# Block 0's expert values weighted on ScalarE and summed on GpSimd, with a fourth tile for its gathered rows

## The chip, the cores and the metric

The kernel runs on one core of a Trainium2 chip. A core has five engines that work side by side, each with its own in-order queue of instructions: TensorE (PE in the profile; its weight loads are PEld), VectorE (DVE), ScalarE (ACT), GpSimd (POOL) and SyncE (SP). SyncE issues the plain DMAs here; GpSimd issues the indirect ones, which gather rows of a table by an index. The metric is the device time of one execution in microseconds, lower is better.

## The reference

One transformer block on 1024 tokens of width 1024, in float32:

```
h  = rmsnorm(x);  x = x + token_mixers(h)      # retention and RWKV-7, gated and merged
h2 = rmsnorm(x);  x = x + peer(h2)             # 16384 experts, 8 heads x 16 chosen a token
x  = x + sigmoid(rmsnorm(x) @ w_gate) * (p @ w_up)
out = rmsnorm(x)
```

The change lies in `peer`. A token's queries give scores against two sets of 128 sub-keys for each head; the best 16 of each set are paired, the best 16 pairs are the head's experts, and a softmax gives their gates. So each token has 128 expert numbers and gates:

```
act = gelu(einsum('td,tkd->tk', h2, expert_u[ids]))     # 128 rows of u for each token
out = einsum('tk,tkd->td', gates * act, expert_v[ids])  # 128 rows of v for each token
```

## The kernel before

Tokens go in eight blocks of 128, a token to a partition. The projections (`project_*`, names Pw, Pr, Pg in the profile), the recurrences (R and T: RWKV pairs and retention, in four units of 256 tokens), the merge of the branches (M), the output matmul (O), the second norm (N) and the queries (F) come in the order of a string in `cfg` (L857). For each block b there are three steps of the expert layer:

- `choose(b)` and `select` (S, L829 to L926): scores are loaded in four parts, two at a time, VectorE takes the best 16 by `max`, `max_index` and `match_replace`, builds the candidates, and picks out the indices with one-hot tiles. Score parts, candidates and one-hots all use the tag `oh` of the pool `sel`, two tiles of 2 KB a partition.
- `dots(b)` (D, L936): for k from 0 to 127 GpSimd gathers row `ids[:, k]` of u into a tile of 4 KB a partition, and VectorE multiplies it with h2 and sums (L956). After the last row the gelu and gates give the weights t.
- what is done with the rows of v: for blocks 0, 6 and 7 `direct()` (G, L988) gathers them in the same way and VectorE adds `t[:, k] * u` to x (L1003), where x starts as the residual. For the other blocks the whole table v is streamed through TensorE against a matrix of the weights (`groups` W, `stream` V).

The gathered rows go round over the tiles that `row(k)` (L975) finds in `self.places`: three in the pool `up` at first; one more (`ux`, L1039) when `open_first` runs, at `<` in the order; two more (`um`, L1021) when the table is streamed. When the stream is over, `values` takes `ux` away again (L1204).

The order string puts the first stage as `[1 x1 S0 r S1 T1 R2 T2 R3 T3 G0 g D1 ]`. `G0` means `dots(0, True)`: D0, then the 128 rows of G0. A planner orders each engine's queue: it takes instructions by their place in the program, those earlier first, when it reckons that what they need is ready. So the rows of D0 and G0 fill gaps between the recurrences R and T, which come before them, and go ahead of the gate projection `g`. `M1 O1 N1 F1` of the next stage follow D1 in the program, and the key choice S2 needs the scores of F1.

At the end, block 7's rows of v are fetched: the first `cfg["ahead"]` of 128 before the last part of the table is streamed (L1185), the others in seven groups, each planned after one of seven tail blocks is done (L1209 to L1211). A tail block (L) is a norm, a matmul with the gate weights `wt`, and the final norm; `wt` is loaded into room that is free when the stream's matrices and the pool of `ux` are closed (`open_tail`, L1230). The tail of block 7 comes last.

```
def row(self, k):
    k %= sum(n for _, n in self.places)
    for pool, n in self.places:
        if k < n:
            return pool.tile([P, D], F32, tag="u", name=self.nm("u"), bufs=n)
        k -= n
```

Of the kernel before, what the change touches and what calls it, by code (L numbers as in the profile page):

```python
# [9 lines left out]
F32 = mybir.dt.float32  # L10
# [10 lines left out]
P = 128  # L21
# [82 lines left out]
class Builder:  # L104
# [724 lines left out]
    def choose(self, b):  # L829

        self.ph = f"S{b}"
        tv = self.sel.tile([P, 8, 2, 16], F32, tag="tv", name=self.nm("tv"), bufs=1)
        ti = self.sel.tile([P, 8, 2, 16], U32, tag="ti", name=self.nm("ti"), bufs=1)
        for h in range(0, 8, 2):
            sc = self.sel.tile([P, 2, 2, 128], F32, tag="oh", name=self.nm("sc"), bufs=2)
            self.q.dma_start(sc, self.scd[b, :, h:h + 2])
            for k in range(2):
                for c in range(2):
                    self.top16(tv[:, h + k, c, :], ti[:, h + k, c, :], sc[:, k, c, :])
        self.select(b, tv, ti)  # L840

    def top16(self, v, i, s):

# [9 lines left out]
    BOXES = [(0, 1, 16), (1, 3, 8), (4, 4, 4), (8, 8, 1)]  # L853
    cfg = dict(nv=5, parts=((0, 256), (256, 768)), mq=0, wp1=(512, 4, 4), mf=((0, 256), (256, 256), (512, 512)),
               wp2=(512, 4, 3), nu=3, nab=3, lag=1, aact=(1, 2), wide=1, hp=(), nmid=1, nmore=2, lb=2, nk=4,
               units=((128, 256), (384, 384)), tail=(0, 1, 2, 6, 3, 4, 5, 7), ahead=64,
               order="[0 c r x0 T0 g k + ] { M0 O0 N0 F0 } [1 x1 S0 r S1 T1 R2 T2 R3 T3 G0 g D1 ] "  # L857
                     "{ M1 O1 N1 F1 ( M2 S2 O2 } < N2 S3 F2 D2 W ) ",
               later=("D3 S4 D4 S5 D5", "S6 S7 G6 G7"))

    def select(self, b, tv, ti):
        self.ph = f"S{b}"
        nc, wk = self.nc, self.sel
        V = nc.vector

        def t(tag, dt, shape=(8, 16)):
            return wk.tile([P, *shape], dt, tag=tag, name=self.nm(tag), bufs=2 if tag == "oh" else 1)

        cand = t("oh", F32, (8, 64))
        o = 0  # L870
        for i0, ni, nj in self.BOXES:
            sh = [P, 8, ni, nj]
            V.tensor_add(cand[:, :, o:o + ni * nj].rearrange("p h (i j) -> p h i j", i=ni),
                         tv[:, :, 0, i0:i0 + ni, None].to_broadcast(sh), tv[:, :, 1, None, 0:nj].to_broadcast(sh))
            o += ni * nj
        tih = t("tih", F16, (2, 16, 8))
        V.tensor_copy(tih, ti.rearrange("p h c n -> p c n h"))
        bv, bp = t("bv", F32), t("bp", I32)
        for h in range(8):
            self.top16(bv[:, h, :], bp[:, h, :].bitcast(U32), cand[:, h, :])  # L880

        m, n = t("m", I32), t("n", I32)
        rank = t("rank", F16, (2, 16, 8))
        turned = [rank[:, c].rearrange("p k h -> p h k") for c in range(2)]
        V.tensor_scalar(m, bp, 3, None, op0=ALU.logical_shift_right)
        V.tensor_scalar(n, bp, 2, None, op0=ALU.logical_shift_right)
        V.scalar_tensor_tensor(m, n, -5.0, m, op0=ALU.add, op1=ALU.max)
        V.scalar_tensor_tensor(m, bp, -47.0, m, op0=ALU.add, op1=ALU.max)
        V.tensor_scalar(turned[0], m, -1.0, 0.0, op0=ALU.add, op1=ALU.max)
        V.tensor_scalar(m, bp, 16.0, -8.0, op0=ALU.is_ge, op1=ALU.mult)  # L890
        V.tensor_scalar(n, bp, 40.0, -4.0, op0=ALU.is_ge, op1=ALU.mult)
        V.tensor_add(m, m, n)
        V.tensor_scalar(n, bp, 56.0, -3.0, op0=ALU.is_ge, op1=ALU.mult)
        V.scalar_tensor_tensor(m, n, 15.0, m, op0=ALU.add, op1=ALU.add)
        V.tensor_tensor(m, bp, m, op=ALU.bitwise_and)
        V.tensor_copy(turned[1], m)

        ijf = t("ijf", F32, (2, 8, 16))
        sh = [P, 8, 16, 8]
        i16 = self.iota16[:, None].to_broadcast(sh)  # L900
        for c in range(2):
            for kk in (slice(0, 8), slice(8, 16)):
                oh = t("oh", F32, (8, 64)).rearrange("p a b -> p (a b)").bitcast(F16)
                oh = oh.rearrange("p (k n h) -> p k n h", k=8, n=16)
                V.tensor_tensor(oh, rank[:, c, kk, None, :].to_broadcast(sh), i16, op=ALU.is_equal)
                V.tensor_mul(oh, oh, tih[:, c, None].to_broadcast(sh))
                for w in (8, 4, 2):
                    V.tensor_add(oh[:, :, 0:w], oh[:, :, 0:w], oh[:, :, w:2 * w])
                V.tensor_add(ijf[:, c, :, kk].rearrange("p h k -> p k h"), oh[:, :, 0], oh[:, :, 1])
        ijf = ijf.rearrange("p c h k -> p c (h k)")  # L910

        gt, s8 = t("gt", F32), t("s8", F32, (2, 8))
        V.tensor_sub(gt, bv, bv[:, :, 0:1].to_broadcast([P, 8, 16]))
        nc.scalar.activation(gt, gt, AF.Exp)
        V.tensor_reduce(s8[:, 0], gt, axis=AX.X, op=ALU.add)
        V.reciprocal(s8[:, 1], s8[:, 0])
        V.tensor_mul(gt, gt, s8[:, 1, :, None].to_broadcast([P, 8, 16]))

        ids = t("ids", I32, (128,))
        V.scalar_tensor_tensor(ids, ijf[:, 0], 128.0, ijf[:, 1], op0=ALU.mult, op1=ALU.add)  # L920
        rows = slice(b * 128, b * 128 + 128)
        self.q.dma_start(self.idsd[rows, :], ids)
        self.q.dma_start(self.gated[rows, :], gt.rearrange("p h k -> p (h k)"))
        self.q.dma_start(self.ijd[rows], ijf)
        self.dump("ids", ids, lambda d: d[rows, :])
        self.dump("gates", gt.rearrange("p h k -> p (h k)"), lambda d: d[rows, :])  # L926
# [61 lines left out]
    def direct(self):  # L988

        b, ids, t = self.gather  # L990
        nc, up = self.nc, self.up
        V = nc.vector
        rows = slice(b * 128, b * 128 + 128)
        table = self.i["peer_v"][0]
        self.ph = f"G{b}"
        x = up.tile([P, D], F32, tag="u_h2", name=self.nm("u_x"), bufs=1)
        self.q.dma_start(x, self.x1d[rows, :])
        for k in range(128):
            self.ph = f"G{b}"
            u = self.row(k)  # L1000
            nc.gpsimd.indirect_dma_start(out=u, out_offset=None, in_=table,  # L1001
                                         in_offset=bass.IndirectOffsetOnAxis(ap=ids[:, k:k + 1], axis=0))
            V.scalar_tensor_tensor(x, u, t[:, k:k + 1], x, op0=ALU.mult, op1=ALU.add)  # L1003
            if k == 127:
                self.dump("x2", x, lambda d: d[rows, :])
                if b == S // 128 - 1:
                    self.x2[b] = x
                else:
                    self.q.dma_start(self.x2d[rows, :], x)
            yield  # L1010
# [290 lines left out]
    def mixers(self):  # L1301
# [6 lines left out]
        for step in self.cfg["order"].split():  # L1308
            op, k = step[0], int(step[1:] or 0)
            with self.tc.high_priority() if step in self.cfg["hp"] else ExitStack():  # L1310
# [15 lines left out]
                elif op == "(":  # L1326

                    self.rctx.close()
                    self.wide = self.cfg["wide"]
                    last = ExitStack()  # L1330
                    self.open_weights(last, self.nm("wp2"), *self.cfg["wp2"])
                    last.push(self.open_big("left"))
                elif op == "<":
                    self.first = self.open_first()
                elif op == ")":
                    last.close()
                elif op == "W":
                    self.build(0, (0,))
                elif op in "]}":
                    pools.close()  # L1340
                elif op == "w":
                    self.project_rwkv()
                elif op == "x":
                    for p in range(4):
                        self.project_rwkv(self.RWKV_CTS[3 * p + (2 if p else 0):3 * p + 5])
                        self.rwkv_pair(k, p)
                elif op == "r":
                    self.project_ret(range(8))
                elif op == "g":
                    self.project_gates(range(16))  # L1350
                elif op == "R":
                    self.rwkv(k)
                elif op == "Q":
                    self.rwkv_pair(k // 10, k % 10)
                elif op == "T":
                    self.retention(k)
                elif op == "M":
                    mT[k] = self.branches(k)
                elif op == "O":
                    xs[k] = self.w_out(k, mT[k])  # L1360
                elif op == "N":
                    h2T[k] = self.norm2(k, xs[k])
                elif op == "F":
                    self.queries(k, h2T[k])
                elif op == "S":
                    self.choose(k)
                else:
                    self.dots(k, op == "G")
        self.pctx.close()
        self.up_ctx = up  # L1370
        return up
# [34 lines left out]
```

## Time and profile before

| | |
|---|---|
| median of 3 runs | 3992.57 us (3992.57 to 3999.76) |
| profiled execution | 4005.58 us, span 4003.8 us |
| TensorE busy | 3216.1 us (80%) |
| VectorE busy | 3067.7 us (77%) |
| ScalarE busy | 984.8 us (25%) |
| GpSimd busy | 1665.9 us (42%) |
| mean granted TensorE clock | 0.884 |
| HBM | 1057.5 MB read, 61.7 MB written, 280 GB/s over the span |

Busy times are summed over the span; they say how full an engine is on average, not what ends last in a stage. The granted clock is a share of full speed. The chain of waits, followed back from the last instruction, gives 20% of the span to "issue", 13% to GpSimd, 13% to DMA, 8% to VectorE and 4% to TensorE. In names, `D0.u` is a gathered row of u for block 0, `G0.u` one of v, `G0.u_x` the sum x.

### The profile page before, as it was taken

How to read it: one execution, taken by the hardware profiler on the slowest of the kernel's cores; microseconds unless marked ns; L12 is line 12 of the kernel's file. 1: busy time of each engine (PE TensorE's matmuls, PEld its weight loads, DVE VectorE, ACT ScalarE, POOL GpSimd, SP SyncE). 2: the span in 40 equal slices, each digit the busy share in tenths (PEclk: the TensorE clock that was granted, in tenths of full speed). 3: DMA queues.
4: the chain of work that ended last, by engine and by line, in shares of the span. 5: the costliest groups of instructions: out<-in, count | busy, mean ns of one | idle time of the engine just before them, and what ended most of it. 6: DMA issues, size and time to landing. Idle time of an engine off the chain costs nothing.

```text
span 4003.8 us, 50659 instructions
## 1 busy us (share of the span) xinstructions
PE 3216.1 (80%) x17036; PEld 2383.0 (60%) x17036; DVE 3067.7 (77%) x7212; ACT 984.8 (25%) x2059; POOL 1665.9 (42%) x1416
## 2 busy tenths in 40 slices
PE   6997768997998876586666975379889998999396
PEld 6886647887888765455554432257654555666142
DVE  5663587886887777687778889989898888676576
ACT  5432342211232210121336001323252222000021
POOL 0000013323233233312554456866537767676442
PEclk8998879998999977798886987589989999999698
DMA  6336548778777768976996999899949999999864
GB/s 193 111 100 189 183 160 260 225 241 262 238 246 228 253 197 272 342 242 225 313 332 211 415 381 357 306 353 409 368 167 369 382 377 383 397 416 395 333 222 163
DMA packets 517257, 1122.57 MB, mean 280 GB/s; under 512 B 42946, under 2 KB 280708, under 8 KB 516996
## 3 DMA queue, kind: packets, MB, share of 16 engines
q0 software_dynamic: 202752, 738.29, 50.8%
q1 hardware_dynamic: 314244, 381.05, 27.6%
q8 instruction: 134, 2.20, 0.2%
q14 instruction: 127, 1.04, 0.1%
HBM read 1057.49 MB, written 61.67 MB: 280 GB/s over the span
## 4 chain that ended last, share of the span: by engine, by line
issue 20%; POOL 13%; DMA 13%; DVE 8%; PE 4%; ACT 0%; SPq 0%; POOLq 0%; DVEq 0%; ACTq 0%
DMA D3.u<-in_peer_u_dram,D3.u_ids 4%; DMA G7.u<-in_peer_v_dram,D7.u_ids 2%; POOL D6.u L954 2%; POOL D7.u L954 2%; POOL D2.u L954 2%; POOL D5.u L954 2%; POOL G6.u L1001 2%; POOL D4.u L954 2%; DVE D3.u L956 1%; DMA D5.u<-in_peer_u_dram,D5.u_ids 1%; PE D7.acc L1164 1%; PE O2.mm L296 1%; POOL G7.u L1001 1%; DMA D4.u<-in_peer_u_dram,D4.u_ids 1%; POOL D1.u L954 1%
## 5 line engine op out<-in xcount | busy, mean ns | idle before, releaser
L1164 PE MATMUL D7.acc<-V1.v,M.M 128*128 128x512 f32 x1536 | 671.1, 598 | 1.3 <-DMA V1.v<-in_peer_v_dram 1.3
L1164 PEld LDWEIGHTS D7.acc<-V1.v,M.M 128*128 128x128 f32 x1536 | 372.9, 244 | 281.9 <-issue 178.4
L1164 PE MATMUL D5.acc<-V0.v,M.M 128*128 128x512 f32 x1024 | 461.2, 611 | 45.7 <-DMA V0.v<-in_peer_v_dram 43.6
L954 POOL DMA_INDIRECT D0.u<-in_peer_u_dram,D0.u_ids x128 | 134.7, 1052 | 827.6 <-DMA D0.u_ids<-idsd 539.5
L1164 PEld LDWEIGHTS D5.acc<-V0.v,M.M 128*128 128x128 f32 x1024 | 251.0, 247 | 245.3 <-issue 130.0
L1001 POOL DMA_INDIRECT G0.u<-in_peer_v_dram,D0.u_ids x128 | 133.5, 1043 | 277.9 <-DVE G0.u_x L1003 197.8
L954 POOL DMA_INDIRECT D2.u<-in_peer_u_dram,D2.u_ids x128 | 143.5, 1121 | 240.6 <-DVE D2.u L956 114.4
L954 POOL DMA_INDIRECT D6.u<-in_peer_u_dram,D6.u_ids x128 | 190.8, 1491 | 123.6 <-DVE K5.raw L1067 38.9
L954 POOL DMA_INDIRECT D1.u<-in_peer_u_dram,D1.u_ids x128 | 131.8, 1030 | 233.1 <-DVE D1.u L956 153.9
L1001 POOL DMA_INDIRECT G7.u<-in_peer_v_dram,D7.u_ids x128 | 151.3, 1182 | 164.1 <-DVE L1.rsq L326 52.0
L1086 PEld LDWEIGHTS <-W0.A 128*128 128x128 bf16 x1536 | 100.7, 139 | 199.3 <-issue 105.7
L956 DVE SCALAR_TENSOR_TENSOR D1.u<-D1.u,D1.u_h 128x1024 f32<-128x1024 f32 x128 | 156.4, 1223 | 78.1 <-DMA D1.u<-in_peer_u_dram,D1.u_ids 72.7
L956 DVE SCALAR_TENSOR_TENSOR D7.u<-D7.u,D7.u_h 128x1024 f32<-128x1024 f32 x128 | 156.4, 1226 | 64.8 <-DMA D7.u<-in_peer_u_dram,D7.u_ids 54.3
L956 DVE SCALAR_TENSOR_TENSOR D0.u<-D0.u,D0.u_h 128x1024 f32<-128x1024 f32 x128 | 155.9, 1221 | 57.2 <-DMA D0.u<-in_peer_u_dram,D0.u_ids 55.2
L954 POOL DMA_INDIRECT D4.u<-in_peer_u_dram,D4.u_ids x128 | 175.5, 1371 | 57.3 <-issue 31.7
L1003 DVE SCALAR_TENSOR_TENSOR G7.u_x<-G7.u,D7.u_t,G7.u_x 128x1024 f32<-128x1024 f32 x128 | 164.5, 1285 | 45.1 <-DMA G7.u<-in_peer_v_dram,D7.u_ids 40.2
L954 POOL DMA_INDIRECT D3.u<-in_peer_u_dram,D3.u_ids x128 | 137.2, 1072 | 147.1 <-DVE D3.u L956 42.9
L1086 PE MATMUL W0.pw<-W0.B,W0.A 128*128 128x64 bf16 x1152 | 80.9, 242 | 143.8 <-DVE W0.B L1132 118.2
L1003 DVE SCALAR_TENSOR_TENSOR G0.u_x<-G0.u,D0.u_t,G0.u_x 128x1024 f32<-128x1024 f32 x128 | 163.9, 1280 | 42.3 <-DMA G0.u<-in_peer_v_dram,D0.u_ids 38.4
L956 DVE SCALAR_TENSOR_TENSOR D2.u<-D2.u,D2.u_h 128x1024 f32<-128x1024 f32 x128 | 156.6, 1226 | 50.2 <-DMA D2.u<-in_peer_u_dram,D2.u_ids 49.7
L954 POOL DMA_INDIRECT D7.u<-in_peer_u_dram,D7.u_ids x128 | 164.4, 1284 | 61.0 <-issue 32.9
L1003 DVE SCALAR_TENSOR_TENSOR G6.u_x<-G6.u,D6.u_t,G6.u_x 128x1024 f32<-128x1024 f32 x128 | 164.4, 1285 | 29.5 <-DMA G6.u<-in_peer_v_dram,D6.u_ids 26.1
(2226 smaller groups left out, 8616.4 us busy)
## 6 DMA issues: line engine op xcount, KB each, us to landing
V0.v<-in_peer_v_dram SPq DMA_DIRECT2D x128, 512.0 KB
V1.v<-in_peer_v_dram SPq DMA_DIRECT2D x128, 512.0 KB
zsd<-Pw256.stage SPq DMA_DIRECT2D x48, 192.0 KB
Pr0.raw<-in_w_in_dram SPq DMA_DIRECT2D x32, 256.0 KB
Pg0.raw<-in_w_in_dram SPq DMA_DIRECT2D x32, 256.0 KB
F0.raw<-in_w_pq_dram SPq DMA_DIRECT2D x32, 256.0 KB
Pr256.raw<-in_w_in_dram SPq DMA_DIRECT2D x32, 256.0 KB
Pg256.raw<-in_w_in_dram SPq DMA_DIRECT2D x32, 256.0 KB
```

The lines of the kernel that those rows point to most:

```text
L296: self.nc.tensor.matmul(out, l, r, start=(j == 0), stop=(j == len(terms) - 1))
L954: nc.gpsimd.indirect_dma_start(out=u, out_offset=None, in_=table, in_offset=bass.IndirectOffsetOnAxis(ap=ids[:, k:k + 1], axis=0))
L956: V.scalar_tensor_tensor(u, u, 1.0, h2, op0=ALU.mult, op1=ALU.mult, accum_out=act[:, k:k + 1])
L1001: nc.gpsimd.indirect_dma_start(out=u, out_offset=None, in_=table, in_offset=bass.IndirectOffsetOnAxis(ap=ids[:, k:k + 1], axis=0))
L1003: V.scalar_tensor_tensor(x, u, t[:, k:k + 1], x, op0=ALU.mult, op1=ALU.add)
L1086: nc.tensor.matmul(pw[:, t * 64:t * 64 + 64], At[:, h * 8 + t], B[:, part, h * 2 + t // 4, :, t % 4], start=(part == 0), stop=(part == 2))
L1164: nc.tensor.matmul(acc[tb][h], w, v[:, h * 512:h * 512 + 512], start=(k == 0 and s == 0 and m == 0), stop=False)
```

## The change

It has four parts:

1. `choose` takes one tile `room` of 4 KB a partition, tag `u` of the pool `sel`, in place of the two `oh` tiles; the score parts, the candidates and the one-hots use its halves by turns.
2. For `G` steps in the order string (only `G0`), `places` gets a fourth tile, that same tag `u` of `sel`, while `dots(0, True)` is laid out, for D0's rows and G0's.
3. In `direct()`, for block 0 alone, ScalarE multiplies the gathered row by its weight in place, and GpSimd adds it to x. Blocks 6 and 7 keep VectorE's multiply-add.
4. `ahead` goes from 64 to 80.

```diff
@@ choose
+        room = self.sel.tile([P, 2, 512], F32, tag="u", name=self.nm("room"), bufs=1)
         for h in range(0, 8, 2):
-            sc = self.sel.tile([P, 2, 2, 128], F32, tag="oh", name=self.nm("sc"), bufs=2)
+            sc = room[:, h // 2 % 2].rearrange("p (k c n) -> p k c n", k=2, c=2)
...
-        self.select(b, tv, ti)
+        self.select(b, tv, ti, room)
@@ cfg
-               units=((128, 256), (384, 384)), tail=(0, 1, 2, 6, 3, 4, 5, 7), ahead=64,
+               units=((128, 256), (384, 384)), tail=(0, 1, 2, 6, 3, 4, 5, 7), ahead=80,
@@ select
-        cand = t("oh", F32, (8, 64))
+        cand = room[:, 0].rearrange("p (h n) -> p h n", h=8)
...
-            for kk in (slice(0, 8), slice(8, 16)):
-                oh = t("oh", F32, (8, 64)).rearrange("p a b -> p (a b)").bitcast(F16)
+            for q, kk in enumerate((slice(0, 8), slice(8, 16))):
+                oh = room[:, 1 - q].bitcast(F16)
@@ direct
-            V.scalar_tensor_tensor(x, u, t[:, k:k + 1], x, op0=ALU.mult, op1=ALU.add)
+            if b:
+                V.scalar_tensor_tensor(x, u, t[:, k:k + 1], x, op0=ALU.mult, op1=ALU.add)
+            else:
+                nc.scalar.activation(u, u, AF.Copy, scale=t[:, k:k + 1])
+                nc.gpsimd.tensor_add(x, x, u)
@@ mixers
-                else:
-                    self.dots(k, op == "G")
+                elif op == "G":
+                    self.places.append((self.sel, 1))
+                    self.dots(k, True)
+                    self.places.pop()
+                else:
+                    self.dots(k)
```

## Rows read from the trace of the kernel before

**Rows 1.** Which engine works in which stretch, the windows view (busy us, instructions, clock, DMA).

```profile
540.00:970.00 430.00, 364.81 (x2447) 332.78 (x2447) 341.03 (x932) 104.66 (x216) 137.09 (x130) 0.94 0.74 239
970.00:1385.00 415.00, 372.87 (x2486) 340.03 (x2486) 322.17 (x611) 114.57 (x221) 132.04 (x127) 0.95 0.76 240
1385.00:1750.00 365.00, 251.06 (x1340) 203.15 (x1339) 252.21 (x549) 57.40 (x116) 130.86 (x127) 0.78 0.83 280
1750.00:1805.00 55.00, 53.64 (x168) 27.55 (x168) 54.42 (x278) 2.85 (x6) 0.00 (x0) 1.00 0.48 156
3795.00:4004.00 209.00, 159.53 (x396) 71.53 (x395) 133.00 (x278) 48.76 (x116) 71.32 (x59) 0.88 0.53 184
```

**Rows 2.** The pass over block 0's values, the view of groups by line.

```profile
L1001 POOL DMA_INDIRECT G0.u<-in_peer_v_dram,D0.u_ids x128 | 133.5, 1043 | 277.9 <-DVE G0.u_x L1003 197.8 <-DMA G0.u<-in_peer_v_dram,D0.u_ids 11.8 <-DVE T2.s L329 9.5
L1003 DVE SCALAR_TENSOR_TENSOR G0.u_x<-G0.u,D0.u_t,G0.u_x 128x1024 f32<-128x1024 f32 x128 | 163.9, 1280 | 42.3 <-DMA G0.u<-in_peer_v_dram,D0.u_ids 38.4 <-DMA G0.u_x<-x1d 3.7
```

**Rows 3.** Three passes' gathers, the tile view (ns least/median/most, first and last start).

```profile
L954 POOL DMA_INDIRECT D0.u<-in_peer_u_dram,D0.u_ids x128: 936/937/1933, 542.1 to 963.3; - x128
L1001 POOL DMA_INDIRECT G0.u<-in_peer_v_dram,D0.u_ids x128: 932/936/2012, 965.3 to 1375.4; - x128
L954 POOL DMA_INDIRECT D1.u<-in_peer_u_dram,D1.u_ids x128: 935/937/1957, 1384.0 to 1740.1; - x128
```

**Rows 4.** Who waited for whom from 965 to 1385 us (us, times, longest), the waits view.

```profile
POOL G0.u L1001 <- DVE G0.u_x L1003: 197.8, 74, 11.4
DVE G0.u_x L1003 <- DMA G0.u<-in_peer_v_dram,D0.u_ids: 38.4, 36, 3.7
```

**Rows 5.** DMA issues by line (kind, count, median us to landing).

```profile
G0.u<-in_peer_v_dram,D0.u_ids POOLq DMA_INDIRECT x128, 5.5
```

**Rows 6.** The nearest rows to a GpSimd add and a ScalarE pass, groups by line.

```profile
L215 POOL MEMSET RB<- 128x512 f32 x4 | 1.9, 520 | 0.3 <-POOLq L1392 0.3
L314 ACT ACTIVATE N1.junk<-O1.x 128x1024 bf16<-128x1024 f32 x2 | 2.1, 1056 | 13.3 <-DVE O1.x L771 11.2 <-issue 2.1
```

**Rows 7.** The chain from 1740 us (start, us, what), and GpSimd's wait after it.

```profile
1740.10 6.20 DMA D1.u<-in_peer_u_dram,D1.u_ids
...
POOL D2.u L954 <- DVE S3.sc L847: 64.2, 1, 64.2
```

**Rows 8.** Retention's stores, the tile view of yd.

```profile
L551 SPq DMA_DIRECT2D yd<-T1.M x2: 370/370/371, 1044.8 to 1077.5; - x2
L551 SPq DMA_DIRECT2D yd<-T3.M x2: 366/366/367, 1571.1 to 1614.0; - x2
```

**Rows 9.** The key choice's first loads and last reads, the tile views of S1.sc and S0.oh.

```profile
L836 SPq DMA_DIRECT2D S1.sc<-scd x4: 319/320/440, 533.8 to 548.3; - x4
L909 DVE TENSOR_TENSOR S0.ijf<-S0.oh x4: 253/271/419, 528.8 to 536.3; 128x64 f32<-128x64 f16 x4
```

**Rows 10.** The end, the timelines of SyncE, VectorE, TensorE, GpSimd (start, us, what, idle before).

```profile
3767.02 2.60 DVE L1003 SCALAR_TENSOR_TENSOR G7.u_x<-G7.u,D7.u_t,G7.u_x 128x1024 f32<-128x1024 f32 x2 [0.22 <-DMA G7.u<-in_peer_v_dram,D7.u_ids]
3769.69 0.38 SPq L1235 DMA_DIRECT2D wt<-in_w_ple_up_dram  x1
3820.36 1.28 DVE L1281 SCALAR_TENSOR_TENSOR L0.o<-L0.x,L0.st,gfin 128x1024 f32<-128x1024 f32 x1
3830.67 1.28 DVE L1003 SCALAR_TENSOR_TENSOR G7.u_x<-G7.u,D7.u_t,G7.u_x 128x1024 f32<-128x1024 f32 x1 [1.03 <-DMA G7.u<-in_peer_v_dram,D7.u_ids]
3834.59 1.30 DVE L1003 SCALAR_TENSOR_TENSOR G7.u_x<-G7.u,D7.u_t,G7.u_x 128x1024 f32<-128x1024 f32 x1 [0.15 <-DMA G7.u<-in_peer_v_dram,D7.u_ids]
3842.92 1.28 DVE L1281 SCALAR_TENSOR_TENSOR L1.o<-L1.x,L1.st,gfin 128x1024 f32<-128x1024 f32 x1
3837.63 0.75 PE L1266 MATMUL L2.pw<-cpers,L2.x 128*128 128x128 f32 x2 [2.80 <-ACT L2.pT L1254]
3763.26 1.02 POOL L1001 DMA_INDIRECT G7.u<-in_peer_v_dram,D7.u_ids  x1 [0.30 <-issue]
3823.11 1.87 POOL L1001 DMA_INDIRECT G7.u<-in_peer_v_dram,D7.u_ids  x1 [51.44 <-DVE L1.rsq L326]
```

More of the change, by code (lines that the diff above doesn't have):

```diff
@@ L859, with select @@
                later=("D3 S4 D4 S5 D5", "S6 S7 G6 G7"))
-    def select(self, b, tv, ti):
+    def select(self, b, tv, ti, room):
         self.ph = f"S{b}"
@@ L866, in t @@
         def t(tag, dt, shape=(8, 16)):
-            return wk.tile([P, *shape], dt, tag=tag, name=self.nm(tag), bufs=2 if tag == "oh" else 1)
-        cand = t("oh", F32, (8, 64))
+            return wk.tile([P, *shape], dt, tag=tag, name=self.nm(tag), bufs=1)
+        cand = room[:, 0].rearrange("p (h n) -> p h n", h=8)
         o = 0
```

## The prediction, made before the result was known

> **What bounds the kernel now.** I read the windows view first [rows 1]. From 540 to 1385 us TensorE is busy for 738 of 845 us at a clock of 0.94 to 0.95, and VectorE for 663. From 1385 to 1750 us nothing is full: TensorE 251 of 365 us at a clock of 0.78, VectorE 252. From 1750 to 1805 us VectorE is full, 54.4 of 55 us, and GpSimd issues nothing. So the first stage is no single engine's. The rows of the two tables come one after another on GpSimd: D0's gathers start at 542.1 and the last at 963.3, G0's run from 965.3 to 1375.4, D1's from 1384.0 to 1740.1 [rows 3]. That is 3.3, 3.2 and 2.8 us a row, though one gather costs GpSimd only 1.04 us [rows 2]. The waits view says why: in G0 GpSimd waits 197.8 us for VectorE to give a tile back, and VectorE waits 38.4 us for rows to land [rows 4]. Three tiles go round; one turn is 3 x 3.2 = 9.6 us, of which 1.0 is the issue, 5.5 the flight [rows 5], 1.3 the multiply-add [rows 2], and the other 1.8 standing in VectorE's queue.
>
> The chain of waits runs through D1's last gather, landing at 1746.3 us, and then through VectorE [rows 7]: behind D1's last rows stand the key choice of block 2 and the merge of unit 2, in the full window [rows 1]. GpSimd waits 64.2 us for them [rows 7] and starts D2 at about 1805 us. From there on gathers follow one another nearly to the end, so I take what moves D2's start to move the end. The question is therefore when D1 ends, and how much VectorE work is left then.
>
> **The change, part by part.** *The fourth tile in D0.* Block 0's rows now go round over four tiles. At an unchanged turn, D0's pitch of 3.32 us [rows 3] falls to 2.49. But VectorE must do 128 x 1.3 = 167 us of D0 beside its other work, 341 - 167 = 174 us in 430 [rows 1], or 0.405 of its time. If it can be busy for 0.93 of the time, my guess below the 0.99 that it reaches from 1750 to 1805 us [rows 1], D0 takes 167/(0.93 - 0.405) = 318 us, not 421. The fourth tile is also taken by the key choice of block 1 until about 590 us. I take 350 us: D0 ends 70 us earlier (bounds 0 and 103).
>
> *G0's multiply-add leaves VectorE.* 164 us of work and 42 us of idle time before it [rows 2] go from VectorE's queue. ScalarE takes 128 passes over 128x1024; its nearest row is 1.06 us [rows 6], 135 us in all, beside 115 busy of 415 [rows 1]: room enough. Its wait for the landing is new, and behind it stand the casts of the gate weights and the PSUM copies for which TensorE waits; VectorE had this wait before (38.4 us [rows 4]), so I count it as exchanged (0; up to +38 if all of it reaches TensorE).
>
> *GpSimd takes 128 adds.* The trace has no GpSimd arithmetic. The nearest row is its memset of 128x512 in 520 ns [rows 6], 1.04 us for 1024 columns, which only writes. That is the lower bound; reading x, reading u and writing one after another is 3.1 us, the upper one. I take two such passes, 2.1 us (two streams in, the writing under them). GpSimd then needs per row 1.04 for the gather [rows 2], 0.30 between instructions [rows 10], 2.1 for the add and some 0.15 for its wait: 3.6 us. It becomes the bound of G0, since a turn of 1.0 + 5.5 + 1.1 + 2.1 = 9.7 us over four tiles is only 2.4. So G0 takes 128 x 3.6 = 461 us where it took 410: +51 (bounds: 2.55 a row, -84; 4.6, +179). The add stands in GpSimd's in-order queue, behind it the next gathers; that is in the pitch. SyncE's store of x waits for the last add as it did for the last multiply-add, with unit 1's weight loads behind it; it moves with G0's end. The Trainium skill, page "GPSIMD Engine Reference", section 3.1, has such an add of 2048 columns at 4497 ns, about twice VectorE's time; by it, as an estimate, 2.25 us here, a pitch of 3.75, and a sum 19 us worse than mine. No run here shows it.
>
> *D1* then starts 70 - 51 = 19 us earlier. It has three tiles as before and keeps its 356 us; it carries -19 to D2's start.
>
> *VectorE's relief.* Retention of unit 1 stores last at 1077.5 and that of unit 3 at 1614.0 us [rows 8]; in between the recurrences of units 2 and 3 run in a chain of short VectorE steps with a 1.28 us multiply-add queued between them. TensorE idles 42 us from 970 to 1385 and 114 us from 1385 to 1750 [rows 1]; a part returns. Work that ends before 1385 also empties the full window behind D1. I take -15 us, no more, since D1's rows stay where they are (bounds 0 and -60).
>
> *The key choice's room.* The halves are used in the old order, so within one choice nothing changes. But one tile is given back only as a whole: the next choice's first load, at 533.8 us while the last use of the tiles before it starts at 536.3 [rows 9], now waits for that end. I take 2.5 us where two choices follow each other on the path (blocks 2 and 3, 6 and 7): +5 (0 to +9).
>
> *ahead from 64 to 80.* The weights of the tail load when the last of the early rows is done: 3767.02 + 2.60 and 3769.69 [rows 10]. They need the room of a tile that takes every sixth row (numbers 3, 9, ...); the last is row 63 of 64 and will be row 75 of 80. Twelve rows at 1.02 + 0.30 us [rows 10] delay the tail by 16 us, in a time in which GpSimd now stands still for 51.4 us [rows 10]. In return the groups between its blocks shrink from 9, 9, 9, 9, 9, 9, 10 rows to 6 and six times 7. The first group's seventh row starts at 3830.67, the ninth at 3834.59, 3.9 us later, and a period is 22.6 us (3820.36 to 3842.92), of which TensorE idles 2.8 [rows 10]. I take 2.8 x 6 and 3 x 1.32 for the last group: -21, so -5 in all (bounds -12, all of 3.9; +12, no shorter period).
>
> Sum: -19 - 15 + 5 - 5 = -34 us. Against the profiled execution, 4005.6 us (span 4003.8), that is 3971.6; that execution is 13.0 us above the median of 3992.6, so I forecast 3992.6 - 34 = 3958.6 us.
>
> **The rivals.** *B, more gain.* The add is at its lower bound or D0 at its limit, and the chain on VectorE shortens well: D1 would end 100 us and more earlier, and then the queries of unit 1 on TensorE hold D2. Of TensorE's 156 us idle half returns, -80, with the tail -85: 3908. For it: 198 us of waits for VectorE [rows 4]. Against it: an add as cheap as a memset.
>
> *C, GpSimd's add is dear.* Place: GpSimd's queue in G0. At 3.1 us the pitch is 4.6, G0 takes 589 us, D1 ends 179 - 70 = 109 us later. GpSimd's pause of 64 us before D2 [rows 7] covers some of it, as far as VectorE gets the key choice done between D1's rows; I count half of it and take off VectorE's relief of 15: 109 - 32 - 15 = +62: 4054. It decides from an add of 2.25 us, where D1 ends as late as before (410 + 70 = 480 = 128 x 3.75); with the pause's half, from 2.5 us. Against it: the value I took lies below, though not by much.
>
> *D, VectorE and GpSimd stand in each other's way.* If an add keeps VectorE's operations on two SBUF tiles waiting, half of the 483 operations beside the multiply-adds [rows 1] meet an add with a chance of 2.1/3.6 and stand for half of one: 240 x 0.58 x 1.05 = 146 us, nearly the 164 that left; the relief is gone, and each add stands some 0.3 us itself: pitch 3.9, G0 +89, D1 +19, with the room and the tail +19: 4012. The trace of before has no GpSimd operation that reads, so it shows neither. The Trainium skill, "SBUF — State Buffer", section "Who interferes with whom", says it of just this pair: a VectorE instruction with two SBUF inputs against a GpSimd instruction that reads, one fully blocked until the other ends. Not shown here.
>
> *E, the fourth tile does nothing.* VectorE, not the tiles, holds D0, whose pitch stays at 3.3: +51 - 15 + 5 - 5 = +36: 4029.
>
> **How the numbers follow.** Forecast 0.43, B 0.17, C 0.13, D 0.13, E 0.06; 0.08 that the terms cancel within 8 us. A measurement here tells 0.2%, some 8 us, from no change. Faster: the forecast and B less 0.01, 0.59. Same: the cancelled case, a part of D and that 0.01, 0.12. Slower: 0.29. The forecast's own range, with an add of 1.9 to 2.3 us and the other terms' bounds, is 3925 to 3985. For 8 in 10 it must take in most of B, D and E: 3895 to 4042; left out are the far ends of B and C.
>
> **What would show it.** D0's last gather near 895 us; GpSimd's adds near 2.1 us, and GpSimd without pauses in G0 at 3.6 us a row; D1's first gather near 1365 and its last near 1720; D2's start near 1770; the tail's weights 16 us later against the last stream, and periods near 20 us. The forecast is wrong if the add is above 2.5 us, if VectorE's short operations grow longer or stand while adds run, if D0 keeps its pitch, or if ScalarE's waits for landings show up as TensorE's idle time.

## The result, and the profile after

The changed kernel takes 4115.3 us (median), the kernel before 3992.6 in the same sets: a ratio of 1.0306, interval 1.0282 to 1.0331, some 122 us slower. 3958.6 was forecast, and the range ended at 4042. The profiled execution is 4109.5 us (span 4107.7), at a mean clock of 0.871 (0.884 before).

The windows view of after, to be read against [rows 1] (busy us and instructions of TensorE, weight loads, VectorE, ScalarE, GpSimd; clock; DMA share; GB/s):

```profile
540.00:970.00 430.00, 377.83 (x2543) 347.38 (x2542) 346.54 (x965) 112.85 (x229) 145.66 (x133) 0.93 0.76 249
970.00:1385.00 415.00, 310.65 (x1857) 280.08 (x1856) 281.72 (x429) 186.81 (x270) 317.65 (x188) 0.81 0.54 169
1385.00:1515.00 130.00, 104.18 (x681) 93.06 (x680) 82.93 (x136) 60.67 (x89) 110.81 (x66) 0.91 0.50 156
```

The first stretch is little changed (TensorE was busy for 365 us). In the second, the one with G0, TensorE does a quarter fewer matmuls (1857, not 2486). VectorE has lost its 128 multiply-adds of 1.28 us and still is busy for 282 us, with only 429 instructions.

The passes of gathers in after, the tile view (ns least/median/most, first and last start), beside [rows 3]:

```profile
L955 POOL DMA_INDIRECT D0.u<-in_peer_u_dram,D0.u_ids x128: 932/938/1978, 546.0 to 950.9; - x128
L1002 POOL DMA_INDIRECT G0.u<-in_peer_v_dram,D0.u_ids x128: 933/952/1424, 953.0 to 1505.4; - x128
L955 POOL DMA_INDIRECT D1.u<-in_peer_u_dram,D1.u_ids x128: 933/937/1974, 1513.8 to 1860.7; - x128
L955 POOL DMA_INDIRECT D2.u<-in_peer_u_dram,D2.u_ids x128: 932/939/1936, 1924.5 to 2239.6; - x128
```

D0 is 16 us shorter, G0 142 us longer. D1 starts 130 us late, D2 119 us late (1805.4 before), and the end of this execution is 104 us late (4107.7, not 4003.8).

GpSimd's adds in after, from the groups by line (busy us, mean ns, idle before and its releasers), and TensorE's longest waits from 970 to 1510 us (total, times, longest):

```profile
L1009 POOL TENSOR_TENSOR G0.u_x<-G0.u_x,G0.u 128x1024 f32<-128x1024 f32 x128 | 304.9, 2382 | 104.1 <-ACT G0.u L1008 93.9 <-DMA G0.u_x<-x1d 8.1
```

```profile
PE R31.pr L665 <- DVE R31.hrw L332: 18.5, 2, 12.4
PE R22.pr L665 <- DVE R22.hrw L332: 10.8, 2, 5.8
```

GpSimd no longer waits for VectorE but 93.9 us for ScalarE, and the add costs 2.38 us. TensorE waits up to 12.4 us for a short VectorE step of the recurrences. The timeline of after shows why (start us, us, what):

```profile
1159.06 0.16 DVE L660 TENSOR_SCALAR R23.hst<-R23.pr 128x4 f32<-128x4 f32 x1
1159.26 2.50 DVE L324 TENSOR_SCALAR R23.hst<-R23.hst 128x4 int32<-128x4 int32 x1
1161.67 0.27 DVE L626 TENSOR_TENSOR R20.ST<-R20.pr,R20.PC 64x128 f32<-64x128 f32 x1
1161.87 0.20 DVE L326 TENSOR_TENSOR R23.rsq<-R23.hst 128x4 f32<-128x4 f32 x1
1162.10 0.17 DVE L327 SCALAR_TENSOR_TENSOR R23.rsq<-R23.rsq,R23.hst 128x4 f32<-128x4 f32 x1
1162.30 2.93 DVE L329 SCALAR_TENSOR_TENSOR R23.hst<-R23.rsq,R23.hst 128x4 f32<-128x4 f32 x1
1165.27 0.16 DVE L326 TENSOR_TENSOR R23.rsq<-R23.hst 128x4 f32<-128x4 f32 x1
```

```profile
1159.34 2.38 POOL L1009 TENSOR_TENSOR G0.u_x<-G0.u_x,G0.u 128x1024 f32<-128x1024 f32 x1
1161.88 0.95 POOL L1002 DMA_INDIRECT G0.u<-in_peer_v_dram,D0.u_ids  x1 [0.16 <-issue]
1162.85 2.35 POOL L1009 TENSOR_TENSOR G0.u_x<-G0.u_x,G0.u 128x1024 f32<-128x1024 f32 x1
```

Two operations on four columns, 0.16 us in before, end when the add ends (1159.34 + 2.38 = 1161.72; 1162.85 + 2.35 = 1165.20). While GpSimd issues a gather, their like go by in 0.17 to 0.20 us. Behind each of the two stands L626, the next link of another recurrence (1161.67 above, and again at 1165.35), and TensorE waits 1.00 and then 2.34 us for it:

```profile
1165.68 0.45 PE L625 MATMUL R20.pr<-R20.ST,R20.FQ 128*64 128x64 f32 x4 [2.34 <-DVE R20.ST L626]
```

### The profile page after: what moved, and what is told of

The parts are those of the page before. It is cut to its first block, busy times and chain, and to the rows that moved or that the text cites. A ratio compares the mean times of both kernels' runs of the same rounds, so it can differ in the third digit from the quotient of the medians.

```text
span 4107.7 us, 50894 instructions
## 1 busy us (share of the span) xinstructions
PE 3236.7 (79%) x17036; PEld 2411.0 (59%) x17036; DVE 3087.4 (75%) x7084; ACT 1119.5 (27%) x2189; POOL 1965.9 (48%) x1544
## 4 chain that ended last, share of the span: by engine, by line
issue 27%; PE 20%; DMA 18%; POOL 16%; DVE 16%; ACT 2%; SPq 0%; POOLq 0%; DVEq 0%; ACTq 0%
DMA D3.u<-in_peer_u_dram,D3.u_ids 3%; POOL D2.u L955 2%; POOL D1.u L955 2%; POOL D6.u L955 2%; POOL D7.u L955 2%; DMA G7.u<-in_peer_v_dram,D7.u_ids 2%; POOL D5.u L955 2%; POOL G6.u L1002 2%; DMA G6.u<-in_peer_v_dram,D6.u_ids 2%; DMA D1.u<-in_peer_u_dram,D1.u_ids 2%; DVE D3.u L957 1%; DMA D5.u<-in_peer_u_dram,D5.u_ids 1%; POOL D0.u L955 1%; DMA D2.u<-in_peer_u_dram,D2.u_ids 1%; POOL D4.u L955 1%
## 5 line engine op out<-in xcount | busy, mean ns | idle before, releaser
L1009 POOL TENSOR_TENSOR G0.u_x<-G0.u_x,G0.u 128x1024 f32<-128x1024 f32 x128 | 304.9, 2382 | 104.1 <-ACT G0.u L1008 93.9
L955 POOL DMA_INDIRECT D6.u<-in_peer_u_dram,D6.u_ids x128 | 180.1, 1407 | 131.8 <-DVE W1.one L1135 44.7
L1094 ACT COPY M.M<-W1.pw 128x512 f32<-128x512 f32 x96 | 79.6, 832 | 417.2 <-PE W1.pw L1092 417.2
L955 POOL DMA_INDIRECT D5.u<-in_peer_u_dram,D5.u_ids x128 | 141.6, 1106 | 101.3 <-DVE D5.u L957 64.9
L1002 POOL DMA_INDIRECT G6.u<-in_peer_v_dram,D6.u_ids x128 | 158.5, 1238 | 65.8 <-DVE G6.u_x L1005 31.3
```

The source lines that it names most:

```text
L1009: nc.gpsimd.tensor_add(x, x, u)
L1094: nc.scalar.copy(self.order(tl, k)[:, tt], pw.rearrange("p (t i) -> p t i", t=8))
```

## The experiments

The theory: VectorE's operations on operands in SBUF stand while GpSimd adds, the recurrences and TensorE's order behind them come late, and that, more than GpSimd's own time, is the loss. Its rivals: GpSimd's longer pass (pitch), ScalarE's queue, and the fourth tile. Each kernel's order of work is planned anew, so differences of times hold the new order as well. In us below, a ratio is multiplied by 3992.6.

**The parts.** The changed kernel with the multiply-add put back:

```diff
-            if b:
-                V.scalar_tensor_tensor(x, u, t[:, k:k + 1], x, op0=ALU.mult, op1=ALU.add)
-            else:
-                nc.scalar.activation(u, u, AF.Copy, scale=t[:, k:k + 1])
-                nc.gpsimd.tensor_add(x, x, u)
+            V.scalar_tensor_tensor(x, u, t[:, k:k + 1], x, op0=ALU.mult, op1=ALU.add)
```

With ahead at 64 as well:

> The room of the key choice and the fourth tile for block 0 alone: block 0's rows of values are weighted and added by VectorE again, and ahead is 64. The theory that the whole loss comes from the pass over G0's rows by ScalarE and GpSimd: D0's last gather at about 950 us as after the change, G0 with four tiles in 380 to 410 us, D1 and all behind it 10 to 45 us earlier than before, so 3950 to 3985 us. Rival, that the fourth tile or the shared room itself costs (later loads of scores, other order of VectorE): 4000 us or more. The step of the prediction (D0 70 us shorter by the tile) would need D0's last gather near 895 us; I no longer expect it.

0.9948 (0.9927 to 0.9968), 3975.7 us. The tile view of it:

```profile
L955 POOL DMA_INDIRECT D0.u<-in_peer_u_dram,D0.u_ids x128: 935/941/1880, 538.6 to 941.6; - x128
L1002 POOL DMA_INDIRECT G0.u<-in_peer_v_dram,D0.u_ids x128: 935/940/1996, 945.3 to 1315.9; - x128
```

The fourth tile pays in G0 (410 to 371 us, more than I had put down), little in D0 (421 to 403). With ahead at 80:

> The whole change without ScalarE and GpSimd: room, fourth tile, ahead 80, with VectorE's multiply-add for block 0. If ahead is worth the 5 us that the tail of the changed kernel showed (353.0 to 347.1 us from G7's first gather to the end), this is 5 to 6 us below the kernel with the tile alone; by the rival, that the shorter tail came from another order of the work and not from ahead, the two are within 2 us.

0.9941 (0.9921 to 0.9961), 3972.2 us; the 3 us to the kernel before it are within the scatter of the sets. The stretch from G7's first gather to the end does tell them apart: 351.3 to 353.0 us in the three kernels with 64, 344.9 to 349.1 in the ten with 80. The engines alone, on the kernel before:

> The kernel before with block 0's rows weighted by ScalarE and added by GpSimd, and nothing else: three tiles, old room, ahead 64. Theory that the loss is the engines' alone: G0's gathers take 540 us or more (three tiles give GpSimd's adds no room to run behind the landings), D1 starts 130 to 200 us later than before, 4110 to 4180 us. Rival, that the fourth tile's turn is what sets the new order and so the loss: D1 starts at most 60 us later, 4040 us or less.

1.0397 (1.0369 to 1.0425), 4150.1 us; G0 557 us. The first theory's numbers came. The engines are the whole loss; room, tile and ahead take some 36 us of it away (1.0397 - 1.0306).

**Whose work.** ScalarE still weights, VectorE adds:

```diff
-                nc.gpsimd.tensor_add(x, x, u)
+                V.tensor_add(x, x, u)
```

> The changed kernel with ScalarE's weighting kept and the add given to VectorE. It takes away GpSimd's 2.38 us a row and whatever its reading does to VectorE, and keeps ScalarE's pass and GpSimd's and TensorE's dependence on its queue. Theory that GpSimd's add is the loss (its own time and VectorE's standing): G0's gathers take 400 to 440 us, and the time is 3970 to 4020 us. Rival, that ScalarE's queue behind landings is the loss (GpSimd waits 93.9 us for it, TensorE's copies stand behind it): G0 still takes 500 us or more, 4070 us or more.

1.0074 (1.0048 to 1.0101), 4023.7 us: just above the first theory's bounds, with G0's gathers (388 us) just below them. From here, GpSimd's add in VectorE's place costs 93 us (1.0306 - 1.0074). But weighting by ScalarE has a price of its own, 53 us over the kernel without it (1.0074 - 0.9941), although VectorE's add of 1.22 us is no longer than the multiply-add of 1.28. The tile view of ScalarE's passes here, with what the engines waited for:

```profile
L1008 ACT ACTIVATE G0.u<-G0.u,D0.u_t x128: 1133/1150/1164, 956.2 to 1336.5; 128x1024 f32<-128x1024 f32 x128
...
  DMA G0.u<-in_peer_v_dram,D0.u_ids: 85.3, 56
```

ScalarE stands 85 us for landings, and TensorE's casts and copies stand in its queue; TensorE is busy for 359 us from 970 to 1385, 378 without the passes. How much of the price is this wait, and how much the 147 us of passes themselves, stays open: passes on data that don't wait for a landing were not tried.

**Pitch or reading.** GpSimd only writes, for 1.92 us a row in place of 2.38 (the sum over block 0's values is left out):

```diff
-                nc.gpsimd.tensor_add(x, x, u)
+                nc.gpsimd.memset(u, 0.0)
+                nc.gpsimd.memset(u, 0.0)
```

> The changed kernel with GpSimd's add replaced by two memsets of the row's tile, 2 x 1.04 us by the row of the memset and so about the add's 2.38 us with the gap between them; GpSimd reads nothing from SBUF, and the sum over block 0's values is left out. GpSimd's time a row stays, the reading goes. Theory pitch (GpSimd's time in G0 makes the loss): G0's gathers take 500 us or more and the time stays above 4080 us. Theory lock (VectorE stands while GpSimd reads, and with it the recurrences, TensorE and ScalarE's queue): VectorE's operations of 128x4 take 0.15 us throughout, TensorE is busy for 350 us or more from 970 to 1385 us (310.7 with the add), G0 takes 450 us or less and the time is 4040 us or less.

1.0057 (1.0033 to 1.0080), 4027.0 us. Each theory had one half: G0's gathers take 534 us, nearly the 552 of after, and the time falls by 99 us all the same (1.0306 - 1.0057). Nor did VectorE's short operations all take 0.15 us (below). The windows view of it, and below it three VectorE groups that read SBUF or PSUM, of after and then of this kernel (from 1000 to 1385 us; x count, busy us, mean ns):

```profile
970.00:1385.00 415.00, 394.04 (x2777) 353.91 (x2775) 232.45 (x600) 229.41 (x345) 289.10 (x306) 0.96 0.62 194
```

```profile
L276 DVE TENSOR_TENSOR Pg256.wlo<-Pg256.raw,Pg256.whi 128x512 fp32r<-128x512 f32 x22 | 22.8, 1044 | 14.4 <-ACT Pg256.whi L275 10.4 <-PE Pg256.mm L304 3.2 <-ACT R20.aa L596 0.9
L527 DVE SCALAR_TENSOR_TENSOR ret_state<-ret_state,cmix 128x128 f32<-128x128 f32 x16 | 15.8, 1045 | 0.0
...
L711 DVE TENSOR_TENSOR R22.X<-R22.pr,cmask 128x512 f32<-128x512 f32 x5 | 3.5, 691 | 3.4 <-PE R22.pr L705 3.4
```

```profile
L276 DVE TENSOR_TENSOR Pg256.wlo<-Pg256.raw,Pg256.whi 128x512 fp32r<-128x512 f32 x26 | 17.9, 690 | 13.7 <-ACT Pg256.whi L275 12.3 <-PE Pg256.mm L304 1.3
L527 DVE SCALAR_TENSOR_TENSOR ret_state<-ret_state,cmix 128x128 f32<-128x128 f32 x16 | 4.6, 346 | 0.0
...
L711 DVE TENSOR_TENSOR R22.X<-R22.pr,cmask 128x512 f32<-128x512 f32 x5 | 3.5, 692 | 5.4 <-PE R22.pr L705 5.4
```

With two operands in SBUF (L276, L527) an operation takes 1.04 us beside adds and 0.69 or 0.35 beside memsets; with one in PSUM (L711) 0.69 either way. All VectorE instructions of the window from 970 to 1385 us average 0.657 us beside adds and 0.387 beside memsets: 0.27 x 429 = some 116 us of standing. The two windows do not hold quite the same operations; line by line against the means of before, the groups add up to some 127 us of standing beside adds and 10 beside memsets. TensorE does 2777 matmuls here, 1857 in after. It idles for 21 us of the 415, in after for 104, and there its granted clock is 0.81, a mean of the levels 1.2 and 2.4 GHz, where it is 0.96 here. What of the loss is the lower clock, and what the waits themselves, was not separated.

The kernels with memsets differ from after in one thing more: the sum x is never written, so SyncE's store of x need not wait for the last add (it goes out at 969 us, not 1514). The waits of SyncE in after show what that can be worth (from 1480 to 1545 us):

```profile
SPq L1015 <- POOL G0.u_x L1009: 3.5, 1, 3.5
SPq L950 <- DMA x2d<-G0.u_x: 2.3, 1, 2.3
```

That is 6 us, and the last recurrence's loads before it in the queue were 161 us later than with memsets already (1484 and 1323 us). Since 1.92 us is less than 2.38, a memset of half a row was added:

```diff
+                nc.gpsimd.memset(u[:, :512], 0.0)
```

> The changed kernel with GpSimd's add replaced by three memsets of the row's tile (1024, 1024 and 512 columns: 0.96 + 0.96 + 0.5 and two gaps, at least the add's 2.38 us); GpSimd reads nothing, the sum over block 0's values is left out. The memsets of 1.92 us gave 4027 us against 4115. Theory lock (VectorE's operations with two tiles in SBUF stand while GpSimd reads): GpSimd's half microsecond more lengthens G0 somewhat, by up to 128 x 0.5 = 64 us less what its waits for ScalarE (153.6 us) take up, and the time is 4025 to 4070 us, well below 4115. Rival, that the shorter GpSimd work explained the gain: 4100 us or more.

1.0140 (1.0096 to 1.0184), 4064.6 us. The tile view and the two groups from above:

```profile
L1002 POOL DMA_INDIRECT G0.u<-in_peer_v_dram,D0.u_ids x128: 932/943/1373, 948.9 to 1561.4; - x128
```

```profile
L276 DVE TENSOR_TENSOR Pg256.wlo<-Pg256.raw,Pg256.whi 128x512 fp32r<-128x512 f32 x23 | 15.8, 687 | 10.1 <-ACT Pg256.whi L275 8.8 <-PE Pg256.mm L304 1.1
L527 DVE SCALAR_TENSOR_TENSOR ret_state<-ret_state,cmix 128x128 f32<-128x128 f32 x16 | 4.6, 346 | 0.0
```

G0's gathers take 612 us, 60 more than in after, and the kernel is still faster than after, by 66 us from the ratios and by 51 from the medians (three of its four runs took 4065 us, one 4037). GpSimd's time does cost: 78 us of G0 cost some 33 us (1.0140 - 1.0057; the interval of 1.0140 is 18 us to either side). But it doesn't explain after.

Now ScalarE's weighting is left out (and so the weights of block 0's values):

```diff
-                nc.scalar.activation(u, u, AF.Copy, scale=t[:, k:k + 1])
```

> The changed kernel without ScalarE's weighting: GpSimd adds the rows as they land (the weights of block 0's values are left out). Theory that ScalarE's queue costs GpSimd its 93.9 us of waits: G0 takes 128 x (0.95 + 0.16 + 2.38 + 0.1) = 460 us and the time is 4020 to 4060 us. Theory that GpSimd's adds cost the time by themselves, and that a wait for ScalarE only stands where another would: G0 takes 520 us or more, 4090 us or more.

1.0401 (1.0370 to 1.0433), 4164.9 us: the first theory has G0 right (457 us) and the time wrong by over 100. The windows view and the waits of D1's gathers in it:

```profile
970.00:1385.00 415.00, 272.74 (x1511) 238.22 (x1509) 331.78 (x344) 72.52 (x140) 394.19 (x235) 0.75 0.60 183
```

```profile
  DVE D1.u L957: 216.7, 99
  DMA D1.u_ids<-idsd: 102.7, 1
```

The denser the adds, the longer VectorE stands: 0.96 us an instruction. TensorE falls to 1511 matmuls, SyncE's queue stands behind the recurrences, and D1, whose ids load in that queue, can't start for 103 us after G0 is done. G0 95 us shorter, the kernel 38 us slower: pitch is refuted as the main price. Half the columns added (the sum over the others is left out):

```diff
-                nc.gpsimd.tensor_add(x, x, u)
+                nc.gpsimd.tensor_add(x[:, :512], x[:, :512], u[:, :512])
```

> The changed kernel with GpSimd adding 512 of 1024 columns of each row (the sum over the other half is left out): some 1.2 us of add a row. GpSimd's pitch could then be 1.0 + 1.2 + 0.4 = 2.6 us, below the 2.9 us that G0 has with the tile alone. If what the add costs is proportional to its time (lock or pitch), G0 takes 400 to 450 us and the time lies near the middle of 4024 (VectorE adds) and 4115: 4030 to 4080 us. If the price is for the dependence on ScalarE and not for the add's time, G0 stays above 500 us and the time above 4090 us.

1.0026 (1.0010 to 1.0043), 4014.9 us, below the 4030 to 4080 that I had put down: with 1.31 us of add G0's gathers take 399 us, and the loss against the kernel before falls from 122 to 10 us. So the price is not proportional to the add's time.

**Versions.** Every fourth row by ScalarE and GpSimd:

```diff
-            if b:
+            if b or k % 4:
```

> The changed kernel with every fourth row of block 0 weighted by ScalarE and added by GpSimd, and the other three by VectorE's multiply-add. If the price goes with the number of GpSimd's adds: 3972 + (4115 - 3972) / 4 = 4008 us. If GpSimd has a share that pays (VectorE relieved of 32 x 1.28 = 41 us, and GpSimd's adds in the time in which it waits for VectorE anyway): 3965 us or less. If handing the sum from engine to engine costs by itself: above 4040 us.

1.0090 (1.0064 to 1.0116), 4034.2 us. None of the three numbers: it is above the share of 4008, and 60 us above the kernel without any. Why a quarter of the adds costs so much stays open, and no other share was tried. The fourth tile for D1 too, with block 0's rows left to VectorE:

```diff
-                elif op == "G":
+                elif op == "G" or op == "D" and k == 1:
...
-                    self.dots(k, True)
+                    self.dots(k, op == "G")
```

> Room, fourth tile and ahead 80 with VectorE's multiply-add, and the fourth tile for block 1's rows of keys (D1) too. With the tile alone GpSimd waits 86 us for the key choice of block 3 behind D1, so the theory that TensorE's unit 2 holds D2 by then has D1 end 20 to 40 us earlier and the time within 8 us of 3972. Rival, that D1's rows still hold VectorE's queue and so the choice: 3940 to 3960 us.

1.0001 (0.9983 to 1.0020), 3994.6 us. Both were wrong. D1's last gather moves from 1683 to 1660, as expected, and D2's first from 1770 to 1793: TensorE's M1 ends later (its last matmul at 1593, not 1538). From 1340 to 1600 us TensorE waits 26 us, not 17, for VectorE's steps of M1, among which D1's rows are now denser, and its granted clock is 0.76, not 0.86; which of the two weighs more is not shown. And ahead 96, also with block 0's rows left to VectorE:

> Room, fourth tile and VectorE's multiply-add with ahead 96 in place of 80. From 64 to 80 the stretch from G7's first gather to the end fell from 351 to 353 us to 346 to 349 us over the kernels that ran. If the next step gives as much: 3968 us and 344 us. If the tail's weights, 16 us later again, hold the first block: 3972 to 3990 us.

0.9999 (0.9976 to 1.0022), 3998.5 us, above the second case's bounds. The stretch from G7's first gather to the end is 366.5 us, 18 more than with 80. The tail's weights load 161 us after that gather, not 135, and the groups between the blocks, 19.1 us with 80, are not shorter any more. The best version again:

> Room, fourth tile and ahead 80 with VectorE's multiply-add once more, in five rounds: it gave 3972.2 us and a ratio of 0.9941 to the kernel before. If that is the gain of the parts without ScalarE and GpSimd, it comes again between 0.992 and 0.997; if it was the scatter of one set of rounds, it lies within 0.2% of 1.

0.9926 (0.9903 to 0.9950), 3970.1 us. The room, the fourth tile and ahead 80, with block 0's rows left to VectorE, beat the kernel before by 0.6 to 0.7%, and the changed kernel by some 3.6%.

**What starts D2.** From the tile views, us (M2 is TensorE's merge of unit 2; S3 the key choice of block 3 on VectorE):

| kernel | G0, first to last gather | D1's last gather | M2's last matmul | S3's first read | D2's first gather | ratio |
|---|---|---|---|---|---|---|
| before | 410 | 1740 | 1801 | 1801 | 1805 | 1 |
| after | 552 | 1861 | 1906 | 1923 | 1925 | 1.0306 |
| tile, ahead 80 | 379 | 1683 | 1766 | 1767 | 1770 | 0.9941 |
| VectorE adds | 388 | 1703 | 1819 | 1821 | 1823 | 1.0074 |
| half the add | 399 | 1716 | 1826 | 1829 | 1831 | 1.0026 |
| two memsets | 534 | 1824 | 1738 | 1854 | 1855 | 1.0057 |
| no weighting | 457 | 1905 | 1952 | 1967 | 1969 | 1.0401 |

Two chains meet at S3: D1's rows, and TensorE's order up to M2. With memsets M2 is done 63 us earlier than before, and D1's rows alone hold D2; with the tile alone M2 does. In after both are late. D2 starts 69 us earlier with memsets than in after: D1 starts 14 us earlier, its rows take 23 us less, and the pause behind them is 32 us shorter.

## Why the prediction was wrong

D1 was to start 19 us earlier and started 130 us later. Of these 149 us, 54 came from D0 and 91 from G0, and 4 from D0's own later start.

*D0's fourth tile: -70 expected, -16 measured (-16 to -23 in the twelve kernels that have it).* This step failed first. I let VectorE be busy for 0.93 of the time if only rows were there; it is for 0.81 (346.5 of 430). GpSimd still waits 182.6 us there for VectorE to give a tile back, while VectorE, idle for 84 of the 430 us, waits only 27.5 us for rows to land (tile view of after, what ended GpSimd's idle time and what VectorE's rows waited for):

```profile
  DVE D0.u L957: 182.6, 85
...
  DVE D0.u L957: 27.5, 24
```

So most rows have landed, and the multiply and sum of such a row stands in VectorE's order behind other operations, of which some wait for other engines. That was rival E's mechanism. G0, to which I gave nothing of the tile, is where it paid when VectorE kept the work.

*G0: +51 expected, +142 measured.* The pitch is 552/128 = 4.31 us, not 3.6. The add is 2.38 us, not 2.1 (+36 over 128 rows), above the 2.25 from which rival C was to decide. The wait for ScalarE is 0.73 us a row, not 0.15 (+74): I had exchanged VectorE's waits for landings against ScalarE's at no price, and never asked what stands ahead of the pass in ScalarE's queue. The pauses between instructions are 16.0 us in all, 0.125 a row and not 0.30 (-22); small terms make the rest of the 91.

*VectorE's relief: -15 expected; it became a loss.* Retention of unit 3 ends on TensorE at 1633, 20 us later than the 1613 of before. With memsets instead of adds it ends at 1425. The relief was far larger than I took, and GpSimd's reading took all of it and more. I had the mechanism as rival D, with 146 us of standing against the 116 to 127 measured in the main window. What failed there is the price behind it: I let it cancel the relief, where it also holds TensorE, whose idle time before VectorE's steps I never carried to M2.

*D2's start follows D1's end.* Half right. The pause between them is 63.8 us in after and was 65.3, so it covered nothing, where rival C counted on half of it. But the row of the full window [rows 1] had TensorE at 53.6 of 55 us beside VectorE's 54.4, and I spoke only of VectorE. M2 ended 4 us before D2's start already; the kernels in which D1 ends 24 to 80 us earlier show M2 holding D2.

*ahead: -5 expected.* Right: from G7's first gather to the end 353.0 became 347.1. In the kernel with the tile and ahead 80 the weights come 135 us after that gather, where it was 119, and a period is 19.1 us, where it was 22.6: the 16 us and the gain in return of the prediction. The room's +5 was not measured alone; with the tile it is more than paid.

So the time lies above every case because C, D and E came together, and I had given each a world of its own.

## What to carry to other kernels

Before work is handed to GpSimd, count not only its time there but, where it reads SBUF, VectorE's operations with two operands in SBUF that will run beside it: each may stand until the GpSimd instruction ends, and what is behind it in order stands too. A pass handed to an engine that feeds TensorE from PSUM brings its wait for the landing into that queue. A further buffer shortens a turn only as far as the engine that gives buffers back can get to them in its order: the same tile was worth 16 to 23 us in D0, and some 30 to 40 in G0 where VectorE kept the work.

## What the runs showed of the hardware

GpSimd's add of two 128x1024 f32 tiles took 2.38 us, of 128x512 1.31; its memset of 128x1024 0.96. The Trainium skill, page "GPSIMD Engine Reference", section 3.1, has 4497 ns for an f32 add of 2048 columns, which led to an estimate of 2.25 us for the first; the measurement, 6% more, decides.

The standing depends on the operands of both. Beside adds VectorE's operations with two SBUF operands grew, in the mean of nearly every such line (L595, 0.41 us, did not). Beside memsets they didn't, but those with a single SBUF operand (L324, L538) did: the timelines of the kernel with two memsets (VectorE, then GpSimd),

```profile
1035.79 0.68 DVE L715 TENSOR_TENSOR R21.M<-R21.M,R21.pr 128x512 f32<-128x512 f32 x1
1036.38 3.49 DVE L538 TENSOR_SCALAR T1.s<-T1.s 128x8 f32<-128x8 f32 x1
1039.91 0.90 DVE L324 TENSOR_SCALAR T1.s<-T1.s 128x8 int32<-128x8 int32 x1
```

```profile
1036.20 1.86 POOL L1009 MEMSET G0.u<- 128x1024 f32 x2
1037.99 1.86 POOL L1010 MEMSET G0.u<- 128x1024 f32 x2
1039.83 0.95 POOL L1009 MEMSET G0.u<- 128x1024 f32 x1
```

have eight columns (0.16 us in before) standing 3.49 us until four memsets are through. The Trainium skill, page "SBUF — State Buffer", section "Who interferes with whom", says both: a VectorE instruction with two SBUF inputs contends with a GpSimd instruction that reads, not with one that only writes, and tensor_scalar in a two-port mode contends with GpSimd altogether, the second comer fully blocked. The runs agree on which operations stand. They do not show that the second comer is the one that stands: by the trace, three of the four memsets began after the VectorE operation that stood for them, and in after L324 began 0.08 us and L329 0.55 us before the add with which they ended (spans on GpSimd are rough). The adds themselves hardly stood: 2.37 us in the middle, 2.92 at most.
